# A mixer and FFN block on Trainium2: hand-written order of ScalarE, VectorE, GpSimd and SyncE in branch A

## The chip, the cores and the metric

The kernel runs on one NeuronCore of a Trainium2 chip. The metric is the device time of one execution in microseconds (us): the median of three runs of the kernel before is 1444.01 us (1442.94 to 1444.41). Five engines work side by side, each through its own instructions in order: TensorE (PE, with its weight loads PEld), VectorE (DVE), ScalarE (ACT), GpSimd (POOL) and SyncE (SP), which issues the DMAs. They wait for one another by semaphores.

## What is computed

One layer of a hybrid encoder, 1024 tokens and 16 meta tokens , model width 1024, in float32. Two attention branches are joined by sigmoid gates; a SwiGLU layer follows. The change is in branch A, the differential attention, and in the gate products that are computed between its steps:

```python
def diff_attn_rows(q1, q2, k1, k2, v, qpos, kpos, key_real, slopes, lam):
    scale = HEAD_DIM ** -0.5
    dist = jnp.abs(qpos[:, None] - kpos[None, :]).astype(jnp.float32) * key_real[None, :]
    bias = -slopes[:, None, None] * dist[None]
    s1 = jnp.einsum('bqhd,bkhd->bhqk', q1, k1).astype(jnp.float32) * scale + bias
    s2 = jnp.einsum('bqhd,bkhd->bhqk', q2, k2).astype(jnp.float32) * scale + bias
    attn = jax.nn.softmax(s1, axis=-1) - lam * jax.nn.softmax(s2, axis=-1)
    return jnp.einsum('bhqk,bkhe->bqhe', attn.astype(v.dtype), v)
...
    proj = h @ w_in
...
    merged = jax.nn.sigmoid(ga) * (y_a @ w_ba) + jax.nn.sigmoid(gb) * (y_b @ w_bb)
    return merged @ w_o
```

`ga` and `gb` are the gate columns of `proj`; `y_a` is normalised per head before `w_ba`.

## The kernel before

Matmuls run on float32 data that is split into two parts of lower precision, high and low; a product takes three matmuls (high by high, high by low, low by high). A split is a copy on ScalarE (high, L117) and a subtraction on GpSimd or VectorE (low, L118).

Branch A goes over 4 heads (h) of 8 query tiles (t) of 128 rows: 32 tiles, counted through as n = 8h + t. A tile has two score matrices (m = 1, then m = 0), each 128 by 1040, computed in three pieces of 392, 392 and 256 columns (`aps`, L814); a piece takes one PSUM bank out of five with the tag "sc". VectorE adds the distance bias to a piece, moves it to SBUF (`as`) and keeps the running minimum (`amn`, L817). After the third piece ScalarE takes Exp with the sum of the row (`adn`, L824); reciprocal (L826); the m = 1 matrix is scaled on GpSimd (L828); VectorE joins the two matrices (L837, "the join") and copies 32 columns (L838). One tile later TensorE transposes the joined matrix in three blocks (`apt`, L849, same banks); ScalarE writes the high part (`at`, L852), VectorE the low part (L853). After every second tile the value products follow (`apy`, L862), after every fourth the normalisation: squares and a scaled copy on ScalarE (L869, L871), sums over columns (`apst`, L875), a power on GpSimd (L878), transposes of the factors (`apf`, L883) and a product on VectorE (L884).

Between these steps TensorE computes the gates: 50 products of 12 matmuls each (`pg`, L751), `gop` being the split operand (four buffers), `gr` its raw form (five). A quarter, three matmuls, is a step. A gate block is a sum of several products at different times: after each product the sum leaves PSUM either as a copy on ScalarE (`gate_stage`, L759, two buffers), or by an addition on VectorE to an earlier sum that was loaded from HBM (`gk`, L756, three buffers); in both cases SyncE stores it (L760) and, where it is needed again, loads it (L636). In this text "gate split" is the making of a `gop`, "gate result" what follows its last matmul.

TensorE's order is written out: a tile has the slots in SLOTS, s for a piece of scores, g for a gate step, n for a part of the values or of the normalisation of an earlier tile, t for a block of transposes of the tile before:

```python
SLOTS = "sgsgsngsgsstntnt"
```

Ahead of each of heads 1 to 3 stand ten gate steps in a row (G_HEAD). The other engines' instructions are put in order by a scheduler, which goes by the order in the program and by when it reckons an operand to be ready; in the first tile alone ScalarE and VectorE have a written order as well. Splits, loads and stores go where the scheduler puts them.

## Time and profile before

| | before |
|---|---|
| median of three runs | 1444.01 us |
| the profiled execution | 1443.88 us |
| its span, first to last instruction | 1442.1 us |
| TensorE clock granted | 0.998 |
| branch A with its gates | about 323 to 619 us |
| ScalarE, Exp (L824), 64 of | 1164 ns |
| VectorE, join (L837), 32 of | 1346 ns |
| VectorE, low part of a block (L853), 64 of | 685 ns |
| GpSimd, low part of a gate split (L118), 47 of | 1406 ns |
| ScalarE, copy of a gate result (L759), 26 of | 580 ns |

Busy times are sums of the instructions' durations; instructions on one engine overlap by about 0.1 us, so the distance from start to start is shorter than the duration. A row of a group or of a timeline gives the line of the kernel, the engine, the operation, output and inputs by the program's names, and shapes; in brackets, or behind the second bar, stands how long the engine was idle before it and who ended that.

### The profile page before, as it was taken

The page shows a single profiled execution, that of the slowest core. Times are in us where ns is not written, and L with a number is a line of the kernel's source. Part 1 is how long each engine was busy: PE and PEld are TensorE (multiplying, and loading weights), DVE is VectorE, ACT ScalarE, POOL GpSimd, SP SyncE. Part 2 cuts the span into 40 slices and gives each one's busy share as a digit, 9 for nine tenths or more (in the row PEclk, how much of TensorE's full clock was granted, in tenths as well). Part 3 has the DMA queues.
Part 4 walks back from the last instruction along what each step waited for, and adds up shares of the span by engine and source line. Part 5 has one row for each costly group of instructions (what it writes and reads, how often), then busy time and mean ns, then how long its engine had stood idle before and what let it go on. Part 6 is the DMA issues. An engine that isn't in the chain of part 4 may idle for free.

```text
span 1442.1 us, 21169 instructions
## 1 busy us (share of the span) xinstructions
PE 1421.4 (99%) x7279; PEld 1219.8 (85%) x7279; DVE 898.4 (62%) x1624; ACT 679.3 (47%) x1290; POOL 644.5 (45%) x605
## 2 busy tenths in 40 slices
PE   8999999999999999999999999999999999999997
PEld 6988989988889989888888788888888888788886
DVE  7468536637787979625514966555555554787567
ACT  6366535546565655545314643333333333444444
POOL 5589227744333433425522775544454442000444
PEclk9999999999999999999999999999999999999999
DMA  8367668996558464586602534333333333964443
GB/s 245 87 211 231 196 160 273 278 286 230 176 177 271 133 220 148 183 258 209 212 22 102 154 99 164 101 105 103 110 100 103 98 109 101 327 207 142 124 129 139
DMA packets 188891, 242.41 MB, mean 168 GB/s; under 512 B 18208, under 2 KB 115936, under 8 KB 188784
## 3 DMA queue, kind: packets, MB, share of 16 engines
q1 hardware_dynamic: 188784, 241.07, 52.9%
q8 instruction: 57, 0.93, 0.3%
q14 instruction: 50, 0.41, 0.1%
HBM read 157.45 MB, written 77.00 MB: 163 GB/s over the span
## 4 chain that ended last, share of the span: by engine, by line
PE 82%; POOL 6%; issue 4%; DVE 4%; DMA 3%; ACT 1%; SPq 0%; POOLq 0%; ACTq 0%; DVEq 0%
PE pg L1328 28%; PE pg L751 8%; PE pd L1422 8%; PE po L1105 6%; PE ppa L796 6%; PE aps L814 4%; PE apy L862 3%; PE pp_qb L214 3%; POOL oa L118 3%; PE pp_ka L214 2%; PE pp_va L214 2%; PE apt L849 2%; PE pp_qa L214 2%; PE bpt L356 1%; PE bpy L362 1%
## 5 line engine op out<-in xcount | busy, mean ns | idle before, releaser
L118 POOL TENSOR_TENSOR wop<-wf,wop 128x512 fp32r<-128x512 f32 x128 | 171.8, 1347 | 166.4 <-ACT wop L117 150.5
L1328 PE MATMUL pg<-t,wop 128*128 128x512 f32 x1056 | 242.6, 389 | 0.0
L1328 PEld LDWEIGHTS pg<-t,wop 128*128 128x128 f32 x1056 | 198.3, 188 | 41.1
L1422 PE MATMUL pd<-ob,oa 128*128 128x512 f32 x924 | 210.7, 390 | 0.8 <-POOL oa L118 0.4
L1422 PEld LDWEIGHTS pd<-ob,oa 128*128 128x128 f32 x924 | 173.2, 188 | 38.2 <-DVE ob L118 1.1
L1328 PE MATMUL pg<-b,wop 128*128 128x512 f32 x792 | 185.6, 392 | 2.4 <-DVE c L1337 2.4
L1328 PEld LDWEIGHTS pg<-b,wop 128*128 128x128 f32 x792 | 149.5, 189 | 34.2 <-issue 2.4
L751 PE MATMUL pg<-hT_hi,gop 128*128 128x512 f32 x384 | 142.3, 395 | 0.0
L118 POOL TENSOR_TENSOR oa<-ra,oa 128x512 fp32r<-128x512 f32 x33 | 44.0, 1336 | 171.2 <-ACT oa L117 169.8
L117 ACT ACTIVATE wop<-wf 128x512 fp32r<-128x512 f32 x128 | 80.2, 631 | 83.2 <-PE pg L1328 48.6
L118 POOL TENSOR_TENSOR gop<-gr,gop 128x512 fp32r<-128x512 f32 x47 | 66.0, 1406 | 106.3 <-ACT gop L117 106.3
L117 ACT ACTIVATE oa<-ra 128x512 fp32r<-128x512 f32 x77 | 48.7, 632 | 106.1 <-PE pd L1422 45.3
L824 ACT ACTIVATE as<-as,amn 128x1040 f32<-128x1040 f32 x64 | 74.5, 1164 | 45.4 <-DVE amn L817 34.4
L1163 DVE TENSOR_TENSOR s<-wf,wf 128x512 f32<-128x512 f32 x22 | 25.5, 1160 | 105.6 <-DMA wf<-in_w_ff_gate_dram 57.7
L814 PE MATMUL aps<-ak,aq 128*128 128x392 f32 (+1 forms) x384 | 89.3, 327 | 1.6 <-DVE amn L817 1.1
L1105 PE MATMUL po<-woh,mT 128*128 128x512 f32 x384 | 88.0, 390 | 0.0
L1105 PEld LDWEIGHTS po<-woh,mT 128*128 128x128 f32 x384 | 71.9, 188 | 14.8
L751 PEld LDWEIGHTS pg<-hT_hi,gop 128*128 128x128 f32 x384 | 72.2, 188 | 11.2 <-DVE gk L756 0.2
L814 PEld LDWEIGHTS aps<-ak,aq 128*128 128x128 f32 x384 | 69.3, 188 | 14.6 <-DVE amn L817 2.0
L343 POOL TENSOR_SCALAR bs<-bs,bdn 128x432 f32<-128x432 f32 (+1 forms) x64 | 41.4, 665 | 85.9 <-DVE bdn L341 74.1
L751 PE MATMUL pg<-hT_lo,gop 128*128 128x512 f32 x192 | 75.8, 395 | 0.0
L828 POOL TENSOR_SCALAR as<-as,adn,neglam 128x1040 f32<-128x1040 f32 x32 | 38.9, 1216 | 57.5 <-DVE adn L826 43.9
(289 smaller groups left out, 3099.4 us busy)
## 6 DMA issues: line engine op xcount, KB each, us to landing
ra<-aop SPq DMA_DIRECT2D x77, 256.0 KB, 2.7
wf<-in_w_ff_gate_dram SPq DMA_DIRECT2D x24, 512.0 KB, 3.9
wf<-in_w_ff_up_dram SPq DMA_DIRECT2D x24, 512.0 KB, 3.9
aop<-as SPq DMA_DIRECT2D x44, 256.0 KB, 2.1
w_c<-in_w_in_dram SPq DMA_DIRECT2D x17, 512.0 KB, 6.1
aop<-c SPq DMA_DIRECT2D x33, 256.0 KB, 2.0
...
```

The costliest lines, as they stand in the source:

```text
L117: nc.scalar.activation(hi, src, AF.Copy)
L118: lo_eng.tensor_tensor(lo, src, f32(hi), ALU.subtract)
L214: nc.tensor.matmul(ps[:, :n], a[:, c, :], b[:, c, at:at + n], start=(c == 0 and i == 0), stop=(c == DC - 1 and i == 2))
L343: nc.gpsimd.tensor_scalar(st[:, r, :W], st[:, r, :W], dn[:, r:r + 1], 1.0, ALU.mult, ALU.mult)
L751: nc.tensor.matmul(ps, op[:, a, c], quad(b, *act)[:, c], start=(p in (2, 5, 1) and c == 0 and i == 0), stop=(p in (2, 3, 4) and c == 3 and ...
L796: nc.tensor.matmul(ps, w[:, a, j, :], src(j, b, tk), start=(j == 0 and n == 0), stop=(j == 3 and n == 2))
L814: nc.tensor.matmul(ps[:, :n], qs[m][:, t * P:(t + 1) * P], ks[m][:, vv, k0:k0 + n], start=(vv == 0), stop=(vv == 1))
L824: nc.scalar.activation(s[m][:, 0:L], s[m][:, 0:L], AF.Exp, bias=low, scale=-1.0, accum_out=dn[:, m:m + 1])
L862: nc.tensor.matmul(py[:, cols], v[:kp, a, k, :], at_[:kp, k, b, :], start=(k == 0 and j == 0), stop=(k == 8))
L1105: nc.tensor.matmul(ps, mT[:, c, a, t * P:(t + 1) * P], wos[q, c][:, b], start=(c == 0 and n == 0), stop=(c == DC - 1 and n == 2))
L1328: nc.tensor.matmul(ps, op[:, x, c, :], b[:, y, c, :], start=(p in (1, 2, 5) and c == 0 and n == 0), stop=(p in (4, 2, 3) and c == 3 and n ...
L1422: nc.tensor.matmul(ps[u], oa[:, a, u * P:(u + 1) * P], ob[:, b, :], start=(p in (1, 2, 5) and j == 0 and k == 0), stop=(p in (2, 3, 4) and ...
```

## The change

All of branch A's instructions on ScalarE, VectorE, GpSimd and SyncE now stand in the order in which the program writes them, and the program is rewritten for it:
- The join of a tile (with its reciprocal) comes behind the next tile's first piece of scores. The low part of the second transposed block follows it; the 32-column copy and the third low part follow the second piece.
- The first Exp of a tile stands behind its third piece, the second behind the first block of transposes.
- The squares and the scaled copy follow the last value matmuls at once.
- A gate split is let go at two places of a tile, behind the first Exp and behind the last block of transposes, or where its product needs it.
- A gate result is taken one step later than before, behind the first three matmuls of the next product. ScalarE itself issues the store of a copied result; that of a sum stays with SyncE. Loads of earlier sums wait for the second step of a product.
- The next head's queries and keys are loaded behind the third and the sixth piece of a head's last tile, its values in its third tile.

TensorE's instructions are the same, in the same order.

```diff
-            kept = g_kept[p, k] = gpool.tile([P, 512], F32, tag="gk", name=f"gk{p}_{k}", bufs=GK_BUFS)
-            nc.sync.dma_start(kept, g_place(p, k))
+            kept_to_do.append((p, k))
+
+    kept_to_do = []
+
+    def load_kept():
+        p, k = kept_to_do.pop(0)
+        kept = g_kept[p, k] = gpool.tile([P, 512], F32, tag="gk", name=f"gk{p}_{k}", bufs=GK_BUFS)
+        nc.sync.dma_start(kept, g_place(p, k))
...
-            return q, k, load_v(h)
...
+    owed = []
+
+    def gate_result(p, k, ps):
+        if p in (1, 6, 7):
+            while (p, k) not in g_kept:
+                load_kept()
+            st = g_kept.pop((p, k))
+            nc.vector.tensor_tensor(st, ps, st, ALU.add)
+        else:
+            st = gpool.tile([P, 512], F32, tag="g", name="gate_stage", bufs=G_BUFS)
+            nc.scalar.copy(st, ps)
+        (nc.sync if p in (1, 6, 7) else nc.scalar).dma_start(g_place(p, k), st)
+        if (p, k) in ((5, 3), (5, 7), (3, 7)):
+            later_p = {(5, 3): 6, (5, 7): 7, (3, 7): 4}[p, k]
+            load_sums(later_p, *G_ACT[later_p])
...
+            while (p, k) not in g_ready:
+                let_go(1)
...
+                while owed:
+                    gate_result(*owed.pop(0))
+                if c == 1:
+                    while kept_to_do and len(g_kept) < GK_BUFS:
+                        load_kept()
                 if c == 3:
-                    if p in (1, 6, 7):
-                        st = g_kept.pop((p, k))
-                        nc.vector.tensor_tensor(st, ps, st, ALU.add)
-                    else:
-                        st = gpool.tile([P, 512], F32, tag="g", name="gate_stage", bufs=G_BUFS)
-                        nc.scalar.copy(st, ps)
-                    nc.sync.dma_start(g_place(p, k), st)
-                    if (p, k) in ((5, 3), (5, 7), (3, 7)):
-                        later_p = {(5, 3): 6, (5, 7): 7, (3, 7): 4}[p, k]
-                        load_sums(later_p, *G_ACT[later_p])
+                    owed.append((p, k, ps))
+                    if n == len(order_g) - 1:
+                        gate_result(*owed.pop(0))
...
-                if i == 1 and behind_first:
-                    behind_first.pop(0)()
                 if i < 2:
                     yield
-            nc.scalar.activation(s[m][:, 0:L], s[m][:, 0:L], AF.Exp, bias=low, scale=-1.0, accum_out=dn[:, m:m + 1])
-            def scaled(m=m):
-                nc.vector.reciprocal(dn[:, m:m + 1], dn[:, m:m + 1])
-                if m:
-                    (nc.gpsimd if t % 4 in COMBINE_POOL else nc.vector).tensor_scalar(
-                        s[1][:, 0:L], s[1][:, 0:L], dn[:, 1:2], neglam, ALU.mult, ALU.mult)
-            if m and n_tile[0] == 0:
-                behind_first.append(scaled)
-            else:
-                scaled()
-            if n_tile[0] == 0:
-                let_go(1)
+            s["low", m] = low
             yield
+
+    def exp_a(s, m):
+        dn = s["of"]
+        nc.scalar.activation(s[m][:, 0:L], s[m][:, 0:L], AF.Exp, bias=s["low", m], scale=-1.0, accum_out=dn[:, m:m + 1])
+
+    def scale_a(t, s):
+        dn = s["of"]
+        nc.vector.reciprocal(dn[:, 1:2], dn[:, 1:2])
+        (nc.gpsimd if t % 4 in COMBINE_POOL else nc.vector).tensor_scalar(
+            s[1][:, 0:L], s[1][:, 0:L], dn[:, 1:2], neglam, ALU.mult, ALU.mult)
+
+    def join_a(s):
+        dn = s["of"]
+        nc.vector.reciprocal(dn[:, 0:1], dn[:, 0:1])
         nc.vector.scalar_tensor_tensor(s[0][:, 0:L], s[0][:, 0:L], dn[:, 0:1], s[1][:, 0:L], ALU.mult, ALU.add)
-        nc.vector.tensor_copy(s[0][:, L:L + 2 * NM].rearrange("p (a k) -> p a k", a=2),
-                              s[0][:, S:L].unsqueeze(1).broadcast_to([P, 2, NM]))
+        behind[1:1] = [lambda: nc.vector.tensor_copy(s[0][:, L:L + 2 * NM].rearrange("p (a k) -> p a k", a=2),
+                                                     s[0][:, S:L].unsqueeze(1).broadcast_to([P, 2, NM]))]
+
+    behind = []
+
+    def catch_up(n):
+        while behind and n > 0:
+            behind.pop(0)()
+            n -= 1
...
-            nc.vector.tensor_tensor(lo, pt[:lo.shape[0], :nb], f32(hi)[:lo.shape[0]], ALU.subtract)
+            def low(lo=lo, pt=pt, hi=hi, nb=nb):
+                nc.vector.tensor_tensor(lo, pt[:lo.shape[0], :nb], f32(hi)[:lo.shape[0]], ALU.subtract)
+            if b:
+                behind.append(low)
+            else:
+                low()
...
-            yield
+            if part < 2:
+                yield
...
-        yg = apool2.tile([P, 512], F32, tag="yg", name=f"yg_{nm}", bufs=2)
+        yg = apool2.tile([P, 512], F32, tag="yg", name=f"yg_{nm}", bufs=1)
         nc.scalar.activation(yg, py, AF.Copy, scale=gsub)
+        yield
...
+    order_av = tc.manual_schedule(engines={mybir.EngineType.Activation, mybir.EngineType.DVE, mybir.EngineType.Pool, mybir.EngineType.SP})
+    order_av.__enter__()
...
+                    ld = ahead
...
+        if n < AH * NT and t == 2 and h:
+            vs[h] = load_v(h)
+        scored = turned = 0
+        if n == AH * NT:
+            catch_up(9)
+            join_a(tiles[n - 1][2])
+            catch_up(9)
         for what in SLOTS if n != 1 else "sgsgsngsgssggtntnt":
-            if what == "s":
-                next(scoring, None)
-            elif what == "t":
-                next(turning, None)
+            if what == "s" and n < AH * NT:
+                next(scoring)
+                scored += 1
+                if scored == 1 and n:
+                    join_a(tiles[n - 1][2])
+                    catch_up(1)
+                if scored == 2:
+                    catch_up(9)
+                if scored == 3:
+                    exp_a(s, 1)
+                    if t == NT - 1 and h < AH - 1:
+                        ahead = load_a1(h + 1)
+                    let_go(1)
...
+                if scored == 5:
+                    scale_a(t, s)
+                if scored == 6 and n == 0:
+                    exp_a(s, 0)
+                if scored == 6 and t == NT - 1 and h < AH - 1:
+                    ahead = load_a0(h + 1, *ahead)
+            elif what == "t" and n:
+                next(turning)
+                turned += 1
+                if turned == EXP_AT and n < AH * NT:
+                    exp_a(s, 0)
+                if turned == 3:
+                    let_go(1)
             elif what == "n":
                 step_tail()
-            else:
+            elif what == "g":
                 fill(1)
...
+    catch_up(9)
+    order_av.__exit__(None, None, None)
```

How rows moved, at three places. In the rows a name's numbers are head, tile and piece or block, and a running number at the end; lines are those of each kernel. First ScalarE, at the start of head 2: `as_1_7` belongs to tile 15, `as_2_0` to tile 16, `gop_1` (with 5441 before, 5456 in the change) is the operand of the third gate product from there. Before:

```order
L852 ACTIVATE at_6_5204<-apt_6_2_5376 128x128
L824 ACTIVATE as_1_3181,adn_7_5292<-as_1_3181,amn_7_5291 128x1040
L117 ACTIVATE gop_0_5422<-gr_0_5399 128x512
L117 ACTIVATE gop_1_5441<-gr_1_5420 128x512
L117 ACTIVATE gop_2_5488<-gr_2_5439 128x512
L824 ACTIVATE as_2_0_5453,adn_0_5452<-as_2_0_5453,amn_0_5451 128x1040
L852 ACTIVATE at_6_5204<-apt_7_0_5513 128x4x128
L824 ACTIVATE as_0_3180,adn_0_5452<-as_0_3180,amn_0_5451 128x1040
L852 ACTIVATE at_6_5204<-apt_7_1_5527 128x4x128
L852 ACTIVATE at_6_5204<-apt_7_2_5534 128x128
```

In the change:

```order
L848 ACTIVATE as_1_3181,adn_7_5282<-as_1_3181,amn_7_5281 128x1040
L881 ACTIVATE at_6_5195<-apt_6_1_5365 128x4x128
L881 ACTIVATE at_6_5195<-apt_6_2_5381 128x128
L848 ACTIVATE as_2_0_5431,adn_0_5430<-as_2_0_5431,amn_0_5429 128x1040
L118 ACTIVATE gop_1_5456<-gr_1_5291 128x512
L881 ACTIVATE at_6_5195<-apt_7_0_5494 128x4x128
L848 ACTIVATE as_0_3180,adn_0_5430<-as_0_3180,amn_0_5429 128x1040
L881 ACTIVATE at_6_5195<-apt_7_1_5509 128x4x128
L881 ACTIVATE at_6_5195<-apt_7_2_5515 128x128
L118 ACTIVATE gop_0_5518<-gr_0_5384 128x512
```

Before, three gate splits stood ahead of the first Exp of tile 16; now the split of `gop_1_5456` stands behind it, and the next one behind that tile's transposes. TensorE's rows of the change at the same place, from the third piece of scores on:

```order
L835 MATMUL aps_0_1_784_5451<-ak_1_5317,aq_1_5315 128x256 x2
L896 MATMUL apy_5_5371<-at_4_4999,av_4823 128x256 x9
L775 MATMUL pg_1_5293<-hT_hi,gop_1_5456 128x512
L775 MATMUL pg_1_5293<-hT_lo,gop_1_5456 128x512
L775 MATMUL pg_1_5293<-hT_hi,gop_1_5456 128x512
L835 MATMUL aps_0_0_0_5475<-ak_0_5316,aq_0_5345 128x392 x2
```

They are those of before but for the running numbers; the product with `gop_1` begins behind nine value matmuls.

Second SyncE at the same place, with the loads of head 2's queries (`aq_1`, `aq_0`) and keys (`ak_1`, `ak_0`); `g_d` are the gate sums in HBM. Before:

```order
L624 DMA gr_2_5439<-in_w_in_dram 128x4x128
L760 DMA g_d_75<-gk_0_4930 128x512
L624 DMA gr_3_5486<-in_w_in_dram 128x4x128
L636 DMA gk_1_5217<-g_d_77 128x512
L671 DMA aq_1_5382<-qa_d_65 128x1024
L664 DMA ak_1_5384<-ka_d_69 128x1040
L666 DMA ak_1_5384<-ka_d_69 64x1040 x2
L677 DMA aq_0_5389<-qa_d_65 128x1024
L664 DMA ak_0_5383<-ka_d_69 128x1040
L666 DMA ak_0_5383<-ka_d_69 64x1040
L760 DMA g_d_77<-gk_1_5025 128x512
```

In the change:

```order
L643 DMA gk_0_5226<-g_d_75 128x512
L625 DMA gr_1_5291<-ws_d_96 128x512
L759 DMA g_d_75<-gk_0_5029 128x512
L643 DMA gk_1_5308<-g_d_77 128x512
L678 DMA aq_1_5315<-qa_d_65 128x1024
L671 DMA ak_1_5317<-ka_d_69 128x1040
L673 DMA ak_1_5317<-ka_d_69 64x1040 x2
L684 DMA aq_0_5345<-qa_d_65 128x1024
L671 DMA ak_0_5316<-ka_d_69 128x1040
L673 DMA ak_0_5316<-ka_d_69 64x1040 x2
```

Before, one load of an earlier gate sum stood ahead of the queries. Now a store of a sum (`gk_0_5029`) and the load of the next (`gk_1_5308`, into the same buffers) stand there.

Third VectorE and ScalarE in tile 18 (`as_2_2`). VectorE before, from the reciprocal of the tile ahead on:

```order
L826 RECIPROCAL adn_1_5541<-adn_1_5541 128x1
L837 SCALAR_TENSOR_TENSOR as_1_3181<-as_1_3181,adn_1_5541,as_2_1_5542 128x1040
L817 ISA as_2_2_5641,amn_2_5639<-aps_2_1_0_5642,dist,far_a 128x392
L817 ISA amn_2_5639 128x1
L853 TENSOR_TENSOR at_0_5450<-apt_0_1_5618,at_0_5450 128x4x128
L838 COPY as_1_3181<-as_1_3181 128x32
L853 TENSOR_TENSOR at_0_5450<-apt_0_2_5632,at_0_5450 16x128
L817 ISA as_2_2_5641,amn_2_5639<-aps_2_1_392_5649,dist,amn_2_5639 128x392
L817 ISA amn_2_5639 128x1
```

VectorE in the change:

```order
L838 ISA as_2_2_5632,amn_2_5630<-aps_2_1_0_5633,dist,far_a 128x392
L838 ISA amn_2_5630 128x1
L858 RECIPROCAL adn_1_5522<-adn_1_5522 128x1
L859 SCALAR_TENSOR_TENSOR as_1_3181<-as_1_3181,adn_1_5522,as_2_1_5523 128x1040
L883 TENSOR_TENSOR at_0_5428<-apt_0_1_5601,at_0_5428 128x4x128
L838 ISA as_2_2_5632,amn_2_5630<-aps_2_1_392_5643,dist,amn_2_5630 128x392
L838 ISA amn_2_5630 128x1
L860 COPY as_1_3181<-as_1_3181 128x32
L883 TENSOR_TENSOR at_0_5428<-apt_0_2_5618,at_0_5428 16x128
L838 ISA as_2_2_5632,amn_2_5630<-aps_2_1_784_5652,dist_m,amn_2_5630 128x256
L838 ISA amn_2_5630 128x1
```

The join moved behind the first piece's reduction, the second block's low part stays behind it, and the copy and the third low part moved behind the second piece's reduction. ScalarE before:

```order
L117 ACTIVATE gop_2_5672<-gr_2_5575 128x512
L824 ACTIVATE as_2_2_5641,adn_2_5640<-as_2_2_5641,amn_2_5639 128x1040
L852 ACTIVATE at_0_5450<-apt_1_0_5697 128x4x128
L824 ACTIVATE as_0_3180,adn_2_5640<-as_0_3180,amn_2_5639 128x1040
L852 ACTIVATE at_0_5450<-apt_1_1_5712 128x4x128
L852 ACTIVATE at_0_5450<-apt_1_2_5719 128x128
L759 COPY gate_stage<-pg_1_5305 128x512
```

ScalarE in the change:

```order
L118 ACTIVATE gop_2_5621<-gr_2_5418 128x512
L848 ACTIVATE as_2_2_5632,adn_2_5631<-as_2_2_5632,amn_2_5630 128x1040
L118 ACTIVATE gop_3_5657<-gr_3_5468 128x512
L758 COPY gate_stage<-pg_0_5208 128x512
L759 DMA g_d_76<-gate_stage 128x512
L881 ACTIVATE at_0_5428<-apt_1_0_5689 128x4x128
L848 ACTIVATE as_0_3180,adn_2_5631<-as_0_3180,amn_2_5630 128x1040
L881 ACTIVATE at_0_5428<-apt_1_1_5705 128x4x128
L881 ACTIVATE at_0_5428<-apt_1_2_5711 128x128
```

Between the first Exp and the high part of the first block a gate split, a copied result and its store came in.

33 lines of the change are left out of this document (12 added, 21 removed).

## The prediction

> **What bounds the kernel now.** First the page: busy time by engine, and the chain that ended last.
>
> ```profile
> PE 1421.4 (99%) x7279; PEld 1219.8 (85%) x7279; DVE 898.4 (62%) x1624; ACT 679.3 (47%) x1290; POOL 644.5 (45%) x605
> PE 82%; POOL 6%; issue 4%; DVE 4%; DMA 3%; ACT 1%; SPq 0%; POOLq 0%; ACTq 0%; DVEq 0%
> ```
>
> TensorE is busy for 99% of the span and carries 82% of the chain. The change leaves its instructions and their order as they are, so it can only alter TensorE's waits, and only in branch A (about 323 to 619 us). So I read the windows of that stage and its groups by shape.
>
> ```profile
> 440.00:480.00 40.00, 40.00 (x246) 36.19 (x244) 33.10 (x96) 21.51 (x39) 16.21 (x13) 1.00 0.77 249
> ```
>
> ```profile
> L814 PE MATMUL aps<-ak,aq 128*128 128x392 f32 x256 | 69.4, 351 | 1.6 <-DVE amn L817 1.1 <-DMA ak<-ka_d 0.5
> L849 PE MATMUL apt<-ident,as 128*128 128x128 f32 x288 | 44.5, 274 | 1.5 <-DVE as L837 1.1 <-DVE amn L817 0.3
> L883 PE MATMUL apf<-ident,af 128*128 128x128 f32 x32 | 4.8, 273 | 0.3 <-DVE amn L817 0.3
> ```
>
> In the window's row the first number behind the bounds is its length, the second TensorE's busy time, the third the weight loads, the fourth VectorE's: nothing is idle on TensorE in 440 to 480, where head 2 starts. By the groups (idle time ahead of them, and who ended it, stand behind the bar) TensorE idles 1.6 + 1.5 + 0.3 = 3.4 us in the whole stage, nearly all behind VectorE. A wait costs a little more than its idle time, since the overlap of neighbouring matmuls is lost too:
>
> ```profile
> 516.88 0.33 PE L849 MATMUL apt<-ident,as 128*128 128x128 f32 x1 [0.96 <-DVE as L837]
> 463.35 0.76 PE L814 MATMUL aps<-ak,aq 128*128 128x392 f32 x4
> 463.94 0.60 PE L849 MATMUL apt<-ident,as 128*128 128x128 f32 x4
> ```
>
> The undisturbed transposes of 463.94 start 0.17 before the scores ahead of them end (463.35 + 0.76); those of 516.88 wait 0.96 behind such an end and lose that overlap besides. With 0.16 more for each of the twelve waits that I find in TensorE's timeline, the stage holds 3.4 + 1.9 = **5.3 us of waits**. That is all the change can win: 1443.88 - 5.3 = 1438.6.
>
> **The change part by part.** Nothing is computed anew; four engines get a fixed order. Tiles are counted through, eight to a head: tile 16 is the first of head 2. I replace the old waits, 5.3, by those that the new order makes.
>
> *The third gate operand of head 2.* In the new order its split stands on ScalarE behind the first Exp of tile 16; before, it stood ahead of it. TensorE takes the operand right after the value matmuls of that tile. These are the rows of the same place before:
>
> ```profile
> 458.21 0.51 PE L814 MATMUL aps<-ak,aq 128*128 128x392 f32 x2
> 461.61 0.39 PE L751 MATMUL pg<-hT_hi,gop 128*128 128x512 f32 x1
> ```
>
> ```profile
> 458.76 0.63 DVE L817 CUSTOM_DVE_ANT_0 as<-aps,dist,far_a 128x392 f32<-128x392 f32 x1 [1.04 <-PE aps L814]
> 460.75 0.48 DVE L817 CUSTOM_DVE_ANT_0 as<-aps,dist_m,amn 128x256 f32<-128x256 f32 x1 [0.30 <-PE aps L814]
> ```
>
> ```profile
> 460.56 0.63 ACT L117 ACTIVATE gop<-gr 128x512 fp32r<-128x512 f32 x1 [2.85 <-PE pg L751]
> 461.33 1.17 ACT L824 ACTIVATE as<-as,amn 128x1040 f32<-128x1040 f32 x1
> ```
>
> ```profile
> 461.27 1.30 POOL L118 TENSOR_TENSOR gop<-gr,gop 128x512 fp32r<-128x512 f32 x1 [2.18 <-ACT gop L117]
> ```
>
> TensorE wants the operand 461.61 - 458.21 = 3.40 us after it starts the first scores. What now lies ahead of it: first scores to VectorE's reduction 0.55; third reduction to Exp 0.58; split's high part to POOL's low part 0.71; low part 1.30. VectorE's steps between, from start to start, and ScalarE's Exp:
>
> ```profile
> 474.77 0.16 DVE L826 RECIPROCAL adn<-adn 128x1 f32<-128x1 f32 x1 [0.72 <-ACT as L824]
> 475.04 1.30 DVE L837 SCALAR_TENSOR_TENSOR as<-as,adn,as 128x1040 f32<-128x1040 f32 x1
> 476.26 0.62 DVE L817 CUSTOM_DVE_ANT_0 as<-aps,dist,far_a 128x392 f32<-128x392 f32 x1
> 476.81 0.69 DVE L853 TENSOR_TENSOR at<-apt,at 128x512 fp32r<-128x512 f32 x1
> 477.41 0.17 DVE L838 COPY as<-as 128x32 f32<-128x32 f32 x1
> 477.49 0.27 DVE L853 TENSOR_TENSOR at<-apt,at 16x128 fp32r<-16x128 f32 x1
> ```
>
> ```profile
> 479.35 1.16 ACT L824 ACTIVATE as<-as,amn 128x1040 f32<-128x1040 f32 x1 [1.53 <-DVE amn L817]
> 480.51 0.57 ACT L852 ACTIVATE at<-apt 128x512 fp32r<-128x512 f32 x1
> 480.99 1.15 ACT L824 ACTIVATE as<-as,amn 128x1040 f32<-128x1040 f32 x1
> 483.21 0.59 ACT L759 COPY gate_stage<-pg 128x512 f32<-128x512 f32 x1 [0.33 <-PE pg L751]
> ```
>
> From start to start: reciprocal 0.27, join 1.22, reduction 0.55, low part 0.60, copy 0.08; the short low part's 0.27 less an overlap of 0.07 gives 0.20, so 0.28 with the copy; Exp 1.16. Sum, in order: 0.55 + 0.55 + 0.27 + 1.22 + 0.60 + 0.55 + 0.28 + 0.58 + 1.16 + 0.71 + 1.30 = 7.77. TensorE is in order and waits 7.77 - 3.40 = **4.4 us**. Nothing hides it: behind the missing operand stand the other scores of the tile and its transposes. The join lies in that chain although its inputs are ready during the ten gate steps ahead of the head.
>
> *Loads of head 2's keys.* Of SP's rows before:
>
> ```profile
> 443.82 0.60 PE L814 MATMUL aps<-ak,aq 128*128 128x392 f32 x2
> ```
>
> ```profile
> 445.15 0.33 SPq L636 DMA_DIRECT2D gk<-g_d  x1
> 446.43 0.33 SPq L671 DMA_DIRECT2D aq<-qa_d  x1
> 447.29 1.09 SPq L666 DMA_DIRECT2D ak<-ka_d  x2
> ```
>
> ```profile
> DMA to landing us min/median/max: 6.0/7.1/12.0
> ```
>
> ```profile
> L760 SPq DMA_DIRECT2D g_d<-gate_stage x25: 319/320/1143, 328.1 to 616.8; - x25
> DMA to landing us min/median/max: 2.0/2.9/10.8
> ```
>
> Now a store of a gate sum and a load into the buffer that this store frees stand ahead of the queries, the load waiting until the store has landed; behind them on SP stand all loads of the head. Tile 15 starts at 443.82. Until the sum is made VectorE needs 0.55 + 0.55 + 0.27 + 1.22 + 0.60 + 0.60 (447.6); issue 0.32, landing 2.0 to 2.9, issue 0.32: the queries go out at 450.3 to 451.1, 3.9 to 4.7 later. The second half of the keys was issued near 448.1 and by the middle landing row came at 455.2; now 459.1 to 459.9 against 458.21. That is 0.9 to 1.7 late; as tile 15's own waits push the need back too, I take 0.7 (bounds 0 and 1.7).
>
> *Loads of head 1.* Issued as before, so the wait for its keys stays: 0.6 (0.5 idle in the group, and the overlap).
>
> *The cycle of a tile.* In the new order one chain runs from tile to tile: Exp, first high part, second Exp, reciprocal, join, low part, reduction, copy with short low part, reduction, Exp: 1.16 + 0.48 + 1.16 + 0.27 + 1.22 + 0.60 + 0.55 + 0.28 + 0.58 = **6.3 us**. A gate split between Exp and high part adds its 0.63 less 0.09 of overlap, 0.54; a copied gate result 0.59 less 0.10, 0.49; its store, now on ScalarE, an issue; a gate sum on VectorE ahead of the second reduction about 0.60, the step of a low part, which reads as much PSUM. Against it stand TensorE's tiles, from first scores to first scores:
>
> ```profile
> 474.31 0.60 PE L814 MATMUL aps<-ak,aq 128*128 128x392 f32 x2
> 480.82 0.60 PE L814 MATMUL aps<-ak,aq 128*128 128x392 f32 x2
> 488.00 0.61 PE L814 MATMUL aps<-ak,aq 128*128 128x392 f32 x2
> ```
>
> ```profile
> 353.56 0.60 PE L814 MATMUL aps<-ak,aq 128*128 128x392 f32 x2
> 359.23 0.60 PE L814 MATMUL aps<-ak,aq 128*128 128x392 f32 x2
> ```
>
> A pair of short tiles has 6.51 + 7.18 = 13.69; tile 4, without values, 5.67. No row shows a DMA issue on ScalarE: the bounds are nothing (ScalarE may run on while the queue works) and the 1.14 of SP's longest; I take SP's median of 0.32, being the same step on another queue.
> - Head 3: 6.3 + 0.54 + 0.60 = 7.44; two pairs lose 2 x 7.44 - 13.69 = 1.2 each: 2.4.
> - Head 2, first pair: 6.3 + 0.54 + 0.49 + 0.32 = 7.65, 1.6 short; some 0.7 is absorbed by the PSUM banks in hand after the long tile ahead: 0.9. Second pair, no split in the chain: 0.2.
> - Head 1: 6.84 a tile, 13.68 a pair: 0; one gate sum in tile 15: 0.5.
> - Head 0: copy and store in nearly every tile, 7.1. Tile 2, without values like tile 4, has its split too: 7.65 against 5.67 lacks 2.0; tile 4 lacks 1.4, less 0.7 in hand; tile 6, 6.51 long, lacks 0.6, in hand: 2.7.
>
> The squares and the scaled copy behind the last values stand on ScalarE between the high parts of a long tile in both orders; that tile's length hides them, and without it they would cost two steps of 0.48 in each of eight places, 7.7. The later loads of the values and the moves on POOL change no row that TensorE waits for: nothing.
>
> The new waits: 4.4 + 0.7 + 0.6 + 2.4 + 1.1 + 0.5 + 2.7 = 12.4. The sum: 1443.88 - 5.3 + 12.4 = **1451.0**. The profiled run lies 0.13 below the median of the runs shown, so this serves as the time. The cycle terms (2.4 + 1.1 + 0.5 + 2.7 = 6.7) may be nil, where the banks absorb them, or double: 1444.3 to 1457.7. A free issue on ScalarE would take some 1.6 of them; one of 1.14 is costlier by 0.82 in head 0's three places and one of head 2, 3.3. SP loses 26 issues; TensorE never waits for one of those stores.
>
> **The rivals.**
> *The banks absorb the cycle.* Scores go to five banks, so VectorE may lag by more than the 0.7 that I allowed; for it speaks that the old stage, whose VectorE is busy 33 of 40 us in 440 to 480, waits nowhere there. Then only the head starts cost: 1443.88 - 5.3 + 4.4 + 0.7 + 0.6 = 1444.3, not slower. It decides if a lag of 1.6, head 2's first pair, is not felt by TensorE.
> *The order does what it says at the head starts too.* If the operand were there in time as well, 1443.88 - 5.3 + 0.6 + 0.7 = 1439.9. Against it stands the 7.77 sum, none of whose steps can be skipped in order.
> *VectorE blocked by POOL.* Rows of two VectorE steps in the cycle:
>
> ```profile
> L837 DVE SCALAR_TENSOR_TENSOR as<-as,adn,as x32: 1279/1301/2237, 334.0 to 587.5; 128x1040 f32<-128x1040 f32 x32
> L838 DVE COPY as<-as x32: 149/164/1152, 335.8 to 589.0; 128x32 f32<-128x32 f32 x32
> ```
>
> They last up to 0.94 and 0.99 above their median. A fixed order sets the join beside POOL's low part of a split; blocked by 0.94 in each of six short places (two each in heads 0, 2 and 3), it costs 5.6 more: 1456.6. [...]
>
> **How the numbers follow.** Forecast (1446.8 to 1456) 0.60; banks absorb (1443 to 1446.8) 0.20; all in time 0.06; blocked (above 1456) 0.14. The range from 1443.0 to 1457.0 takes in the bounds of the cycle terms and leaves out the third case and half of the last. About 0.2%, 2.9 us, is what a measurement here tells from no change: faster 0.06 (the third case), within 0.22 (the second, and a little of the first), slower 0.72.
>
> **What would show it.** In the profile after: one TensorE wait of over 4 us on POOL's gate operand in tile 16, its start at about 3.4 us behind the first scores; a wait of under 2 us for keys just before; no wait on the join (L837 of before), which leaves the list of releasers; instead many waits of 0.2 to 1.2 us on VectorE's reductions and low parts in heads 0, 2 and 3. No wait in tile 16, or heads 0 and 3 without waits, would make the forecast wrong.

## The result and the profile after

| | before | after |
|---|---|---|
| median | 1443.99 us | 1460.98 us |
| lowest to highest of four runs | 1442.94 to 1444.41 | 1460.08 to 1465.43 |
| ratio, with its 95% interval | | 1.0123 [1.0111, 1.0136] |

The change costs 17 us. The profiled execution is the slowest of the four (1465.43, 21.6 above the one before): it lost 4.2 us at 112 to 118 us, behind a copy on VectorE that lasted 6.11 us in this execution and 1.30 in the one before, in code that the change doesn't touch and at a place where no other profile of this study waits. Positions below are those of this execution, differences are taken inside branch A alone.

The page after has, as its busy times and its chain:

```profile
PE 1431.4 (98%) x7279; PEld 1221.0 (83%) x7279; DVE 899.1 (61%) x1624; ACT 675.6 (46%) x1290; POOL 645.2 (44%) x605
PE 50%; issue 5%; POOL 4%; ACT 1%; DVE 0%; DMA 0%; POOLq 0%; ACTq 0%
```

The same 7279 matmuls, and none of the other engines is busy for over 1 us more. So the time is in TensorE's waits, or in its clock. (The chain can be followed back only to 570.87 us here, so its shares don't compare with those of before.) The window of 440 to 480, after:

```profile
440.00:480.00 40.00, 34.73 (x195) 29.61 (x194) 25.51 (x72) 15.76 (x31) 9.85 (x9) 0.97 0.76 248
```

TensorE was busy for all 40 us of it before; now it stands for 5.27, and the granted clock (the last but two) fell from 1.00 to 0.97. The waits of TensorE in branch A by what it waited for: us in all, times, longest.

```profile
PE aps L835 <- DVE amn L838: 3.8, 10, 0.5
PE pg L775 <- ACT gop L118: 2.8, 1, 2.8
PE aps L835 <- DVE at L883: 2.1, 5, 0.7
PE pg L775 <- ACT gate_stage L758: 1.8, 1, 1.8
PE aps L835 <- DMA ak<-ka_d: 1.3, 1, 1.3
PE pg L775 <- POOL gop L119: 0.6, 1, 0.6
PE apt L878 <- DVE at L883: 0.2, 1, 0.2
```

That is 12.6 us of idle time in 20 waits against 3.4. The waits on the join are gone, as forecast. What stands there now is of two kinds: four waits at the starts of heads 1 and 2, up to 2.8 us, and sixteen short ones on VectorE's reductions and low parts.

To see the whole price I take each matmul's distance to the one before it, and subtract the distance that the same pair had before the change. Over branch A the differences add up to 19.3 us:

| where | us |
|---|---|
| head 2: third gate operand (two waits) | 3.8 |
| head 2: keys | 1.4 |
| head 1: copied gate result | 1.9 |
| half clock behind these waits, at heads 1 and 2 | 1.7 + 1.8 |
| short waits, heads 0 to 3 | 4.0 + 1.6 + 2.3 + 4.4 |
| differences of under 0.1 each | 1.1 |
| waits of before that went | -4.7 |

Behind branch A 2.2 come back, 1.1 at each of two places. At the first TensorE waits 2.0 us for VectorE in both profiles, and only in the one before half a clock follows; the row of before, then that of after:

```profile
831.00:833.00 2.00, 2.00 (x7) 1.56 (x6) 2.00 (x5) 0.18 (x1) 0.00 (x0) 0.53 0.03 8
853.00:855.00 2.00, 1.31 (x6) 1.13 (x7) 2.00 (x3) 1.11 (x2) 1.08 (x1) 1.00 0.03 8
```

**Head 2.** TensorE's timeline there, with ScalarE's:

```profile
468.43 0.33 PE L835 MATMUL aps<-ak,aq 128*128 128x392 f32 x1
470.02 0.42 PE L835 MATMUL aps<-ak,aq 128*128 128x392 f32 x1 [1.26 <-DMA ak<-ka_d]
472.26 1.24 PE L896 MATMUL apy<-at,av 128*128 128x256 f32 x9
476.33 0.50 PE L775 MATMUL pg<-hT_hi,gop 128*128 128x512 f32 x1 [2.83 <-ACT gop L118]
477.68 0.61 PE L775 MATMUL pg<-hT_hi,gop 128*128 128x512 f32 x1 [0.62 <-POOL gop L119]
479.17 0.63 PE L775 MATMUL pg<-hT_lo,gop 128*128 128x512 f32 x1
```

```profile
474.50 1.16 ACT L848 ACTIVATE as<-as,amn 128x1040 f32<-128x1040 f32 x1 [11.15 <-DVE amn L838]
475.66 0.61 ACT L118 ACTIVATE gop<-gr 128x512 fp32r<-128x512 f32 x1
```

The first Exp starts as soon as VectorE's third reduction is done, and the split stands behind it. From the first scores (468.43) to the matmul that needs the low part (477.68) are 9.25 us: within 0.1 the 7.77 of the prediction's sum and the 1.4 for which the keys were late. Of the wait of 4.4 that this makes, the two matmuls that need only the high part use some 0.6 (they run from 476.33 on), which leaves 3.8.

The last row shows what the prediction left out: this matmul takes 0.63 us instead of 0.40. The windows of the same place, of 2 and 1 us, the granted clock standing third from the end:

```profile
474.00:476.00 2.00, 0.00 (x0) 0.00 (x0) 0.41 (x3) 1.50 (x3) 0.00 (x0) 1.00 0.79 266
478.00:479.00 1.00, 1.00 (x4) 0.90 (x3) 0.00 (x0) 0.00 (x0) 0.00 (x0) 0.50 0.72 221
```

From 477.92 on TensorE gets half its clock for 3.4 us: matmuls start every 0.43 us instead of 0.23. That adds 1.8 us to the price of this wait; not every wait of its length is followed by it (last section).

**Head 1.** ScalarE's rows (ACTq is its DMA issue), and TensorE's one and the window behind it:

```profile
388.55 0.33 ACTq L759 DMA_DIRECT2D g_d<-gate_stage  x1
391.72 0.59 ACT L758 COPY gate_stage<-pg 128x512 f32<-128x512 f32 x1
395.40 0.33 ACTq L759 DMA_DIRECT2D g_d<-gate_stage  x1
397.72 0.58 ACT L758 COPY gate_stage<-pg 128x512 f32<-128x512 f32 x1 [5.41 <-DMA g_d<-gate_stage]
```

```profile
398.36 0.50 PE L775 MATMUL pg<-hT_hi,gop 128*128 128x512 f32 x1 [1.79 <-ACT gate_stage L758]
```

```profile
400.00:402.00 2.00, 2.00 (x9) 1.80 (x8) 1.20 (x6) 0.22 (x1) 0.00 (x0) 0.50 1.04 394
```

Here the keys and queries of head 1 are in flight (DMA share 1.04). The store behind the first copy, now ScalarE's, stands from 392.3 to 395.4. The next copy needs one of two staging buffers, and waits until the store of 388.55 has landed, 9.1 us after its issue; the gate step that needs that copy's bank waits for it, and half a clock follows here too. Before, a copy waited nearly as long at this place, with no TensorE wait behind it:

```profile
395.16 0.59 ACT L759 COPY gate_stage<-pg 128x512 f32<-128x512 f32 x1 [5.21 <-DMA g_d<-gate_stage]
```

**The short waits.** The starts of three tiles of head 3, and POOL and VectorE between them:

```profile
561.20 0.60 PE L835 MATMUL aps<-ak,aq 128*128 128x392 f32 x2
568.41 0.63 PE L835 MATMUL aps<-ak,aq 128*128 128x392 f32 x2 [0.33 <-DVE amn L838]
576.81 0.61 PE L835 MATMUL aps<-ak,aq 128*128 128x392 f32 x2
```

```profile
568.37 1.29 POOL L119 TENSOR_TENSOR gop<-gr,gop 128x512 fp32r<-128x512 f32 x1 [3.12 <-DVE amn L838]
569.64 1.22 POOL L853 TENSOR_SCALAR as<-as,adn,neglam 128x1040 f32<-128x1040 f32 x1
```

```profile
570.90 1.30 DVE L859 SCALAR_TENSOR_TENSOR as<-as,adn,as 128x1040 f32<-128x1040 f32 x1 [0.77 <-POOL as L853]
572.72 0.68 DVE L755 TENSOR_TENSOR gk<-pg,gk 128x512 f32<-128x512 f32 x1
```

The pair of tiles takes 7.21 + 8.40 = 15.61 us, where the prediction had 2 x 7.44 = 14.88; before, this pair took 13.75. The chain has the forecast steps and one more: the join also needs the scaled matrix from POOL, which now stands behind the low part of the split, and waits 0.77 for it. Such waits of the join come nine times, 5.7 us in all; before there was none.

### The profile page after: what moved, and what is told of

Read it like the earlier page. It is cut to its first block, busy times and chain, and to the rows that moved or that the text cites. A ratio compares the mean times of both kernels' runs of the same rounds, so it can differ in the third digit from the quotient of the medians.

```text
span 1463.4 us, 21152 instructions
## 1 busy us (share of the span) xinstructions
PE 1431.4 (98%) x7279; PEld 1221.0 (83%) x7279; DVE 899.1 (61%) x1624; ACT 675.6 (46%) x1290; POOL 645.2 (44%) x605
## 4 chain that ended last, share of the span: by engine, by line
PE 50%; issue 5%; POOL 4%; ACT 1%; DVE 0%; DMA 0%; POOLq 0%; ACTq 0%
PE pg L1388 26%; PE pd L1482 9%; PE ppa L818 6%; PE po L1165 6%; POOL oa L119 3%; PE pg L775 2%; POOL wop L119 1%; PE apy L896 1%; ACT t L118 0%; DMA wf<-in_w_ff_gate_dram 0%; PE apt L878 0%; POOL t L119 0%; ACT wop L118 0%; POOL as L853 0%; PE aps L835 0%
## 5 line engine op out<-in xcount | busy, mean ns | idle before, releaser
L835 PE MATMUL aps<-ak,aq 128*128 128x392 f32 (+1 forms) x384 | 93.6, 337 | 7.8 <-DVE amn L838 3.8
L883 DVE TENSOR_TENSOR at<-apt,at 128x512 fp32r<-128x512 f32 (+1 forms) x96 | 52.5, 549 | 17.4 <-ACT at L881 17.1
```

What stands on the lines that cost most here:

```text
L835: nc.tensor.matmul(ps[:, :n], qs[m][:, t * P:(t + 1) * P], ks[m][:, vv, k0:k0 + n], start=(vv == 0), stop=(vv == 1))
L883: nc.vector.tensor_tensor(lo, pt[:lo.shape[0], :nb], f32(hi)[:lo.shape[0]], ALU.subtract)
```

## The experiments

The kernel before ran beside each, with medians of 1443.5 to 1444.7; ratios are to it, with 95% intervals. Expectations for parts of the change count from 1460.6, one of the four times of the changed kernel.

### Splits at a head's start earlier

```diff
-                fill(G_HEAD if h else G_FIRST)
+                for _ in range(G_HEAD if h else G_FIRST):
+                    fill(1)
+                    if h:
+                        let_go(9)
```

> Only change: during the ten gate steps ahead of each of heads 1 to 3, held-back gate splits are let go after every step, so the third operand of head 2 is split before that head's first Exp. Theory (long waits and what follows them): the 3.8 us wait on the operand in tile 16 goes, and so does the half granted clock behind it (about 1.8 us): 1460.6 - 5.6 = 1455.0. Rival 1 (the half clock has another cause, for instance the wait for keys just before): 3.8 alone goes, 1456.8. Rival 2 (the wait moves to the next operand or sum): 1459 to 1461.

1461.57 us, 1.0125 [1.011, 1.014]: nothing won. TensorE and VectorE in this kernel, at the same place:

```profile
475.15 0.33 PE L878 MATMUL apt<-ident,as 128*128 128x128 f32 x1 [2.69 <-DVE amn L838]
```

```profile
473.86 0.69 DVE L755 TENSOR_TENSOR gk<-pg,gk 128x512 f32<-128x512 f32 x1 [4.99 <-DMA gk<-g_d]
```

The wait for the operand is gone, and another of nearly its length was right behind it: VectorE stands for an earlier gate sum that has not been loaded, with the tile's reductions queued behind it. The changed kernel has that wait of VectorE as well, hidden by TensorE's own:

```profile
479.70 0.69 DVE L755 TENSOR_TENSOR gk<-pg,gk 128x512 f32<-128x512 f32 x1 [5.29 <-DMA gk<-g_d]
```

### Filler in the long wait

Sixteen matmuls are added ahead of the late operand of head 2; they write the bank of the tile's next scores, taken early for this, and their result is overwritten.

```diff
+                if "ps" in s:
+                    for _ in range(16):
+                        nc.tensor.matmul(s["ps"], s['ks'][1][:, 0, 0:P], quad(0, 0, 1)[:, 0], start=True, stop=True)
```

> Adds 16 matmuls of 512 columns (3.7 us) on TensorE just ahead of the product that waits for the late operand in tile 16; they write a score bank that the next scores overwrite, so nothing that is computed changes. Theory (the clock is halved because TensorE idled): the wait is filled with work, the granted clock stays 1.0 behind it, and the matmuls from 478 on take 0.23 us instead of 0.43: 1460.6 - 1.8 = 1458.8, with more work done. Rival (the half clock has nothing to do with the wait): 1460.6, and 0.5 granted at the same place.

1459.84 us, 1.0108 [1.0093, 1.0123]. TensorE's row of the filler, and the windows behind it:

```profile
468.43 3.88 PE L1018 MATMUL aps<-hT_hi,ak 128*128 128x512 f32 x16
```

```profile
472.00:474.00 2.00, 1.97 (x10) 1.36 (x9) 0.00 (x0) 0.00 (x0) 0.75 (x1) 1.00 0.47 149
474.00:476.00 2.00, 2.00 (x17) 1.96 (x16) 1.28 (x4) 0.58 (x1) 0.00 (x0) 1.00 0.93 294
```

Up to 478 no window has a granted clock under 1.00, and from 464 on TensorE gains 2.1 us on the changed kernel (0.8 of it is given back by 487). The filler ends within 0.1 us of where the waits for the operand would have ended, so it gains nothing there. 0.65 of the gain is a shorter wait for keys, which the edit doesn't explain; the other 1.5 lies behind the filler, where matmuls start 0.23 us apart instead of 0.43, and is the half clock. In the whole time the intervals of the two kernels overlap; the effect is read from the rows of one execution. That it isn't luck, the count in the last section supports: without the filler some 2.8 us of idle time, an estimate from the wait of 2.83 in the changed kernel, would have fallen into one step of the clock's grid (468.05 to 471.46 in this execution), more than any step had that kept the full clock (1.89 at the most).

### Transfers: keys ahead, or SP left to the scheduler

In the first kernel loads of earlier sums are held back until the next head's keys are issued.

```diff
-                    while kept_to_do and len(g_kept) < GK_BUFS:
+                    while kept_to_do and len(g_kept) < GK_BUFS and not hold_kept[0]:
...
+        hold_kept[0] = n < AH * NT and t == NT - 1 and h < AH - 1
...
+                        hold_kept[0] = False
```

> Only change: in the last tile of a head, loads of earlier gate sums are held back until the loads of the next head's queries and keys are issued. Theory: head 2's queries go out about 3 us earlier and its 1.4 us wait for keys goes: 1459.2. Rival (the 16 DMA engines are full there, share 1.0, so that an earlier issue lands no earlier): 1460.6. If the half clock hangs on the two waits of tile 16 together, it may go as well: 1457.4.

1466.21 us, 1.0161 [1.0144, 1.0178]. The wait for keys is gone; VectorE and TensorE show what came instead:

```profile
469.90 0.69 DVE L755 TENSOR_TENSOR gk<-pg,gk 128x512 f32<-128x512 f32 x1 [9.85 <-DMA gk<-g_d]
```

```profile
476.35 0.80 PE L775 MATMUL pg<-hT_hi,gop 128*128 128x512 f32 x1 [9.47 <-ACT gop L118]
```

The later load holds VectorE for 9.85 us, and with it the reductions, the Exp, and the split behind the Exp. In the second kernel SP has no written order:

```diff
-    order_av = tc.manual_schedule(engines={mybir.EngineType.Activation, mybir.EngineType.DVE, mybir.EngineType.Pool, mybir.EngineType.SP})
+    order_av = tc.manual_schedule(engines={mybir.EngineType.Activation, mybir.EngineType.DVE, mybir.EngineType.Pool})
```

> Only change: SyncE is taken out of the written order, so the scheduler places loads and the stores of sums again; ScalarE, VectorE and GpSimd keep their order, and copied results are still stored by ScalarE. Theory (SyncE's written order delays keys and earlier sums at the heads): the 1.4 us wait for head 2's keys goes and VectorE's 5.3 us wait for an earlier sum shrinks: 1460.6 - 1.4 = 1459.2; the operand's wait stays. Rival (landing is slow because the 16 engines are full, whatever the order): 1460.6.

1462.04 us, 1.0126 [1.0109, 1.0143]: no difference. Again no wait for keys, and 5.08 us for the operand, behind a VectorE that stood 5.45 for a load.

### The split behind the second Exp

```diff
                 if scored == 3:
                     exp_a(s, 1)
-                    let_go(1)
...
                 if turned == EXP_AT and n < AH * NT:
                     exp_a(s, 0)
+                    let_go(1)
```

> Only change: the first of a tile's two gate splits is let go behind the second Exp instead of behind the first. Theory (the chain from Exp to Exp is the bound in short tiles, and 0.54 of it is the split): the small waits in heads 2 and 3, some 6 us in sum, shrink by 0.5 a short tile: -3 to -4, but the late operand in tile 16 comes some 2 us later still and its half clock stays: 1460.6 - 3.5 + 2.0 = 1459.1. Rival (the chain is not the bound, the banks are): the small waits stay, 1462.6.

1469.18 us, 1.0185 [1.0145, 1.0224]. TensorE's waits on reductions and low parts fall from 5.9 to 3.4 us (in 9 places instead of 15), and the second tile of head 3's pair takes 7.44 us instead of 8.40: there the split does lengthen the chain from tile to tile. Over the whole stage that isn't shown, since a TensorE that stands elsewhere also waits less here: operands now come late in eight places, 11.3 us.

### Early splits with four buffers for earlier sums, four for raw operands

```diff
-GK_BUFS = 3
-GR_BUFS = 5
+GK_BUFS = 4
+GR_BUFS = 4
```

(with the early splits of the first experiment)

> Early splits at the heads as in e1_split_early, and four buffers for earlier sums (raw operands have four instead of five, for room). Theory (in e1 TensorE's wait moved to VectorE, which stood behind an earlier sum whose load waited for a buffer): with the fourth buffer the load goes out before, the 2.7 us wait of e1 and its half clock go: 1461.6 - 2.7 - 1.8 = 1457.1. Rival (the load is late because the DMA engines are full): 1461.

1470.9 us, 1.0186 [1.0165, 1.0207], slower by more than the changed kernel: 7.7 us of waits on reductions, 5.3 on copied results, 2.7 on operands.

### One more part undone alone, or two

Copied results stored by SP:

```diff
-        (nc.sync if p in (1, 6, 7) else nc.scalar).dma_start(g_place(p, k), st)
+        nc.sync.dma_start(g_place(p, k), st)
```

> Only change: SyncE issues the stores of copied gate results too, as before the change; everything else keeps the new order. Theory (at the start of head 1 a store on ScalarE's queue waits until a load of head 1's queries has landed, 392.3 to 395.4, and the copy behind it until a store has landed, to 397.7; TensorE waits 1.95 us for that copy and then runs at half clock): ScalarE no longer stands behind the load, the copy comes about 3 us earlier, the wait and the half clock go: 1460.6 - 3.6 = 1457.0, and head 0's chain is 0.3 a tile shorter: 1456. Rival (the copy's own wait for a buffer is what counts, whoever issues): 1460.6. Second rival: SyncE, in order, now stands behind the copies and brings head loads later: over 1461.

1463.43 us, 1.0142 [1.0116, 1.0167]: no gain in all. In head 0 there is one: TensorE's waits fall from 2.3 us in seven places to 1.1 in two. Heads 1 and 2 lose it again. The copies at head 1 wait 7.6 and 7.7 us for their buffers, and TensorE 5.0 us in all for keys; SP, in its written order, now stands for copies too, up to 7.3 us.

Results taken at once:

```diff
-                    owed.append((p, k, ps))
-                    if n == len(order_g) - 1:
-                        gate_result(*owed.pop(0))
+                    gate_result(p, k, ps)
```

> Only change: a gate result is taken right behind the last matmul of its product, not one step later. Theory: copies and sums start 0.7 us earlier in TensorE's terms, so stores land earlier: up to 0.7 each of head 1's 1.95 and head 2's waits, 1459.2; but ScalarE and VectorE, in order, now stand up to 0.5 us behind TensorE's last matmul in many tiles, which lengthens the chain: rival 1462.

1461.0 us, 1.0117 [1.0094, 1.014]: none either. Waits on reductions fall from 3.8 to 2.2 us, and the operand of head 2 is waited for 4.5 instead of 2.8.

Early splits and stores on SP together:

> The new order with SyncE issuing all stores and with splits let go during the gate steps ahead of a head. Against e10_repaired it keeps SyncE's written order and the late results. Theory: the operand's wait is replaced by VectorE's behind an earlier sum, as in e1_split_early, and head 1's wait goes as in e8_store_sync: 1457. Rival: both stay, 1461.

1463.37 us, 1.0135 [1.0113, 1.0157]: both kinds of wait stay, 4.3 us on keys and 2.3 behind VectorE at the transposes.

### Four repairs together

Splits early at heads, results at once, stores on SP, and SP left to the scheduler: the edits above. ScalarE, VectorE and POOL keep their written order.

> ScalarE, VectorE and GpSimd keep the new order; SyncE is left to the scheduler and issues all stores, gate results are taken at once, and splits are let go during the gate steps ahead of a head. Theory (the waits of 1.4 us and more at heads 1 and 2, and the half clocks behind them, come from these four): 10.6 us go (1.95 + 1.7 + 1.4 + 3.8 + 1.8), and the small waits of the chain stay: 1460.6 - 10.6 = 1450.0. Rival (VectorE in order still stands behind a late earlier sum at head 2, 2.7 us and a half clock): 1454.5.

**1447.83 us**, 1.0028 [1.0016, 1.004]: 13 of the 17 us are back. What TensorE still waits for:

```profile
PE aps L833 <- DVE amn L836: 1.8, 6, 0.5
PE apt L876 <- DVE amn L836: 1.4, 1, 1.4
PE aps L833 <- DMA ak<-ka_d: 1.2, 1, 1.2
PE aps L833 <- DVE at L881: 0.9, 2, 0.7
```

Four parts that each win nothing alone win 13 us together. So I took each one back from this kernel.

*Stores on ScalarE again:*

> The repaired kernel (1447.8) with one repair taken back: the copied results are stored by ScalarE again. Theory (the written order of SP and the late splits do the damage, the store on ScalarE only passes it on): once SP's loads are placed in time, ScalarE's store waits for nothing, so 1448 to 1450. Rival (ScalarE's queue blocks by itself: 5.4 us behind the store's landing beside head 1, of which TensorE saw 1.95 and half a clock window of 1.9): 3 to 4 us more than repaired, 1451 to 1452, with a wait of TensorE on a copy of L758 above 1 us.

1450.04 us, 1.0033 [1.002, 1.0045]: not to be told from the repaired kernel. ScalarE's copies still wait up to 3.5 us for their buffers, and TensorE for none of them.

*Late splits again:*

> The repaired kernel (1447.8) with one repair taken back: the operands at a head's start are split in their late place again, behind the first Exp of the new head's first tile. Theory (late splits cost by themselves: at head 2 a wait of 3.8 us and half a clock window of 1.8, as in the changed kernel): 1452 to 1454, with one wait of TensorE on a gate operand above 3 us in tile 16. Rival (the split was late only since SP's order kept its load and the engines ahead of it waiting): no wait on an operand above 1 us, 1447 to 1449.

1456.33 us, 1.0076 [1.005, 1.0102]. The wait, foreseen at 3.8, is 8.4:

```profile
473.27 0.79 PE L775 MATMUL pg<-hT_hi,gop 128*128 128x512 f32 x1 [8.38 <-ACT gop L118]
```

The sum on VectorE (4.85 behind its load, at 470.26) stands in front of the Exp, and the split behind it: the two lengths add.

*Results a step late again:*

> The repaired kernel (1447.8) with one repair taken back: a gate result is again taken a step late, behind the next group of matmuls. Theory (only the position on the vector engines moves, which is not what TensorE waits for): 1447 to 1449. Rival (a late sum stands ahead of a tile's reductions on VectorE, 0.68 us each and up to 5 us where its load is late): 1450 to 1453, with waits of TensorE on reductions (amn) of 4 us or more in all against 3.2 in the repaired kernel.

1455.44 us, 1.0074 [1.0053, 1.0096]. The rival's waits are there: 5.1 us on reductions in all against 3.2, since the late sum stands in the chain ahead of a reduction; the pair of tiles of head 3 takes 15.64 us again, against 14.60 in the repaired kernel. But the longest wait is one that neither theory named. TensorE and ScalarE:

```profile
392.56 0.50 PE L775 MATMUL pg<-hT_hi,gop 128*128 128x512 f32 x1 [3.06 <-ACT gate_stage L758]
```

```profile
391.92 0.59 ACT L758 COPY gate_stage<-pg 128x512 f32<-128x512 f32 x1 [6.67 <-DMA g_d<-gate_stage]
```

That is the changed kernel's wait at head 1, now with the stores on SP, so it doesn't need ScalarE's queue. The late result is not its only source: with results at once and SP in its written order, 1.2 us of it stay (0.8 with early splits and stores on SP besides). Whether a third staging buffer would take it away no run shows; with one, this written order deadlocks.

*SP in written order again:*

> The repaired kernel (1447.8) with one repair taken back: SP issues its transfers in the written order again. Theory (SP's order is the main cause: its loads stand behind waits of loads and stores ahead of them): most of the 13 us comes back, 1458 to 1463, with a wait of TensorE on keys or behind a late sum of 2 us or more. Rival (with the splits early and the results at once, SP's order no longer matters): 1447 to 1450.

1455.63 us, 1.0079 [1.0053, 1.0105]: some 7 of the 13 us, less than foreseen. TensorE waits 4.8 us for keys, at head 2 and at head 3:

```profile
467.61 0.42 PE L833 MATMUL aps<-ak,aq 128*128 128x392 f32 x1 [1.66 <-DMA ak<-ka_d]
539.42 0.42 PE L833 MATMUL aps<-ak,aq 128*128 128x392 f32 x1 [1.64 <-DMA ak<-ka_d]
```

So three of the four parts carry some 6.5 to 7.5 us each (ratio less 1.0028, by 1444), the store on ScalarE none that shows. These add up to some 21, more than the four win together. The rows of head 2 show how that can be: in the changed kernel VectorE's 5.3 us for a load lay under TensorE's wait for the operand and cost nothing more, and with the splits alone late the two stand one behind the other, 8.4 us.

### What is left, and a version to keep

What the repaired kernel still loses is at the start of head 2, where VectorE stands 4.8 us for an earlier sum. Three kernels on top of it, and one of two together:

*POOL left to the scheduler too:*

> The repaired kernel (1447.8) with POOL left to the scheduler too, so that only ScalarE and VectorE keep the written order. What is left of the loss there (3.8 us) lies at the start of head 2, where VectorE stands 4.8 us behind a sum whose earlier result arrives late, and a half clock window follows. Theory (that late arrival is the whole rest, POOL's order plays no part): 1447 to 1449. Rival (POOL's written order holds split operands and raw buffers, and so the transfers): 1444 to 1446, with the wait behind the sum below 3 us.

1446.58 us, 1.0016 [1.0003, 1.0028]: between the two cases, the interval overlapping that of the repaired kernel. The join waits for POOL no longer (5.2 us before), the sum still 4.7. The pair of tiles of head 3 takes 14.25 us instead of 14.60.

*The cycle's split behind the second Exp:*

> The repaired kernel (1447.8) with the split of each tile's cycle behind the tile's second Exp instead of its first (at the heads' starts still early). Theory of the chain (the split of 0.6 us between the first Exp and the second lengthens the way from a tile's scores to its low parts; the waits on reductions and low parts, 2.7 us there, fall to about 1): 1445.5 to 1447. Rival (operands then come late in other tiles, as in the kernel that only moved the split): waits on gate operands above 3 us in all and 1451 to 1460.

1452.45 us, 1.0063 [1.0048, 1.0078]: TensorE waits 3.5 us for operands, and 3.3 on reductions and low parts, where about 1 was expected; moving the split doesn't pay here either.

*Four buffers for earlier sums, four for raw operands:*

> The repaired kernel (1447.8) with four buffers instead of three for the earlier results that the sums add to, and four instead of five for raw operands. Theory (the rest of the loss is the load of an earlier result at head 2, which waits up to 3.4 us for the store before it to free its buffer): the wait of 4.8 us behind the sum falls below 1.5, the half clock window goes, 1443 to 1445.5, level with the kernel before. Rival (raw operands with one buffer fewer come late): 1451 to 1460, with waits of TensorE on gate operands above 3 us.

**1444.26 us**, 1.0004 [0.9994, 1.0014]: level with the kernel before. All waits of TensorE in the stage, and head 2's window:

```profile
PE aps L833 <- DVE amn L836: 1.6, 6, 0.5
PE aps L833 <- DVE at L881: 1.2, 3, 0.7
```

```profile
466.00:468.00 2.00, 2.00 (x14) 1.88 (x14) 1.47 (x7) 1.85 (x6) 1.02 (x1) 1.00 0.53 180
```

The wait for the load has left VectorE's list, the half clock with it. In the changed kernel with early splits alone the same edit cost time (1470.9 against 1461.6), with waits on operands and copied results that are not there now.

*Both of the last that helped:*

> The repaired kernel with four buffers for the sums (1444.3) and POOL left to the scheduler as well. Theory (the two gains add up: POOL's order cost 1.2 us in the repaired kernel): 1442.5 to 1443.5, level with the kernel before or a little under it. Rival (POOL's order cost only through the late sum at head 2, which the fourth buffer has taken away): no difference, 1443.7 to 1445.

1442.67 us, 0.9993 [0.9983, 1.0004]: the lowest median of the study, with ScalarE and VectorE in the change's order; that it beats the kernel before is not shown.

## Why the prediction was wrong

The direction was right and the time 10 us too low, above the range. The step that failed is the sum of the new waits: 12.4 us forecast, 24.0 measured (12.3 of short waits, 7.1 of waits at the heads, 3.5 of half clock behind them, 1.1 in differences too small to place). By its steps:

- *Waits of before*: 5.3 forecast, 4.7 measured. The waits on the join went.
- *Third gate operand of head 2*: right in place, length of its chain (7.77) and cause; 4.4 against 3.8, since two matmuls need the high part alone.
- *Keys of head 2*: 0.7 against 1.4, inside its bounds. *Loads of head 1*: 0.6 against no wait.
- **The price of a long wait** was taken as its idle time and a lost overlap of 0.16. Missing is the half clock that can follow: 1.7 and 1.8 us here, shown by the windows at 0.50 and by the filler. That both waits were followed by it is in part luck: a wait of 2.0 us behind branch A was not, in the same execution.
- **"Its store, now on ScalarE, an issue"**, and "TensorE never waits for one of those stores". I priced the issue (0.32; it took 0.33), and not what the copies of head 1 stand for in order: stores that land late, with two buffers. Before, ScalarE waited there nearly as long, and the result was taken early enough that TensorE never saw it; taken a step later, it cost 1.9 and half a clock window. The prediction read the change's "one step later" as a place in the order of VectorE and ScalarE, not as a PSUM bank that is freed later.
- **The cycle terms**, 6.7 against 12.3 of short waits: right in mechanism and places, the size of the cycle wrong. The forecast has no term for POOL's branch of it, the scaled matrix behind the low part of the split, 0.77 in the row of head 3. The pair there lost 1.9, not 1.2, and later kernels show how this is shared: it takes 15.61 us in the changed kernel, 14.60 in the repaired one, where the gate sum is taken at once (15.64 with that part alone taken back), 14.25 with POOL left to the scheduler too, and 13.75 before. So 1.0 is the late sum in the chain, for which the forecast had 1.2 in the pair; some 0.4 is POOL's order, whose moves the forecast put at nothing ("change no row that TensorE waits for"), and 0.5, which had no term either, stays open. In the whole stage the waits on VectorE fall from 5.4 to 2.7 us with the results at once in the repaired kernel, and 2.0 of these 2.7 lie in head 3. In head 0 either of two parts undone alone takes about half of the waits away, the store on ScalarE or the late result.

The rivals: the banks don't absorb the cycle, and the head starts were not in time. The measured time lies where *VectorE blocked by POOL* would have put it (above 1456), but this did not come: all 32 joins took 1300 to 1303 ns, sixteen of them beside a low part of a split on POOL.

```profile
L859 DVE SCALAR_TENSOR_TENSOR as<-as,adn,as x32: 1300/1301/1303, 337.8 to 612.6; 128x1040 f32<-128x1040 f32 x32
L119 POOL TENSOR_TENSOR gop<-gr,gop x47: 1272/1297/2108, 335.3 to 633.3; 128x512 fp32r<-128x512 f32 x47
```

In this order the join always started first, and POOL's instruction beside it was the one that stretched: fifteen of the sixteen took 1.50 to 2.11 us (the other, 1.29, began 0.08 before the join's end), against a median of 1.30. In the profile before too it was the later of the two. Four low parts that had started ahead of a join took 1.28 to 1.30 us and the joins beside them 1.32 to 2.24; eight that started behind one took 1.55 to 2.34, and those joins 1.28 to 1.30. One of the four:

```profile
348.26 1.29 POOL L118 TENSOR_TENSOR gop<-gr,gop 128x512 fp32r<-128x512 f32 x1 [1.86 <-ACT gop L117]
348.91 1.74 DVE L837 SCALAR_TENSOR_TENSOR as<-as,adn,as 128x1040 f32<-128x1040 f32 x1
```

The waits at the heads were each priced from one view of before, in which something else hid them. What the prediction lacked is the next thing late behind each: the sum on VectorE that lay under the operand's wait (5.29 us, felt by TensorE only when the operand came early), and the stores under the copies.
